# A delta net's projection fed without its norm factor, beta / |k|^2 moved into the decay's exponent, seven small transfers for fourteen

## The chip, the cores and the metric

One core of a Trainium2 chip runs the whole program. The metric is the time of one execution in device microseconds, as the median of three: 1213.83 before the change (1212.03 to 1216.12). The change touches the first 200 of these microseconds almost alone: the first layer, a gated delta net.

## The reference, cut to what matters

Two transformer blocks run one after the other over 256 tokens of 1024 features in fp32. Only the first layer of the first block matters here:

```
hn  = x * rsqrt(mean(x^2) + eps) * a_norm_w              # rmsnorm, one factor per token
q, k, v, z, b, a = split(hn @ a_w_in)                    # 1024, 1024, 2048, 2048, 16, 16 columns
q, k, v = silu(causal_conv4(q, k, v))                    # four taps along the tokens
q, k    = q / |q| * 128^-0.5, k / |k|                    # 8 heads, used by 16 value heads
beta, g = sigmoid(b), -exp(a_log) * softplus(a + dt_bias)
gc      = cumsum(g);  decay[c, s] = exp(gc[c] - gc[s])   # c >= s, inside a chunk of the tokens
m       = strict_lower(beta[c] * (k[c] . k[s]) * decay)
T       = inverse(1 + m)                                 # lower triangular
...                                                      # T and the products q.k, k.v make the outputs o
h       = x + (rmsnorm(o) * silu(z)) @ a_w_out
```

The factor of the norm is one number per token, so that (x * a_norm_w) @ W, times that number per token, is the projection too. In the same way |k|^-2 and beta are factors of m, and a positive factor of an exponential is a summand, its logarithm, in the exponent.

## The kernel before, in words

**Matmuls.** Features lie on the 128 partitions and tokens along the free axis, so the input is eight pieces of 128 features by 256 tokens. A product in fp32 is made of three matmuls in a faster format: each operand is split into a high half (a rounded copy) and a low half (what the rounding left), and high by high, low weight by high x and high weight by low x are summed in a PSUM bank (`mm3`, L247 to L251). All weights stream in as 362 chunks of 128 x 1024 (`wall[j]`), each of eight tiles of 128 x 128 in the order in which TensorE uses them. `_raw` issues a chunk's transfer on SyncE's queue, `_prep` makes the high half `wh` on ScalarE (L186) and the low half `wl` on VectorE (L187). There are four buffers of each kind, and `w` prepares two chunks ahead.

**Order.** The engines' orders are static. A scheduler makes them from the order in which the code issues the instructions and from priorities: the splits of the weights have a high one. `behind` adds an order between two instructions of an engine by hand. Work that isn't part of a weight loop runs in generators: `tick` (L200) advances each of them by one step for every four weight tiles that were used. A finished PSUM bank is evacuated by `evac`; while `ready` is false the evacuations wait in a queue, `evq`, and `flush` issues them.

**The start of the delta net (`gdn`, L547 to L574).** The input arrives in four transfers of two pieces (`h`), then the identity, chunk 0 and the table of small columns. ScalarE squares, VectorE sums, TensorE sums over the partitions (`colsum`, L361), VectorE takes the reciprocal root (`rstd`), TensorE spreads it over all partitions (`rows`). Then each piece is multiplied by a_norm and by the factor (L568), split into `xh` on ScalarE (L569) and `xl` on VectorE (L570), and the projection starts. Nine matmuls without use (`warm`) fill waits of TensorE.

**The projection.** First come two groups of k columns together, piece by piece (`ko=2` in `gemm`), then the 48 columns of b and a, the other two groups of k, and then by the table `ORDER` four groups of q, four blocks of z and eight groups of v. A group is a bank of two times 128 columns by 256 tokens. Its evacuation `conv` (L642 to L651) is one copy times the last tap's weight on ScalarE, three taps on VectorE for each half, each reading the bank, and a Silu on ScalarE. `evac_ba` (L605 to L628) makes beta and the running sums of g: Tanh, Exp and Ln on ScalarE and small operations on VectorE; its `later` turns them over into `bg`, with the tokens on the partitions.

**The decay.** `factors` makes 1/|k| and, in `negc`, -beta/|k|^2 (L685). `x_stage` (L692 to L720) then takes each of eight key heads: two matmuls make the products `kk` in three blocks of 128 columns (two in the first half of the tokens, one in the second), and for each of its two value heads two matmuls make the exponents in a bank `rp`, ScalarE takes three Exp with gc as the bias (L704 to L706), and VectorE multiplies `kk`, `negc` and the Exp in two instructions (L707, L708). Diagonal blocks go out to DRAM, come back in another shape, `inv_stage` inverts them in 31 steps on VectorE, and fourteen small transfers (L770, L773, all on SyncE) bring the results back. `levels` builds the whole inverse from them, and `chain` the outputs. `a_stage` (L732, L733) makes the products of q and k as `x_stage` does those of k.

Of the kernel before, what the change touches and what calls it, by code (L numbers as in the profile page):

```python
# [19 lines left out]
P = 128  # L20
# [92 lines left out]
WARM = (5, 1, 3)  # L113
# [19 lines left out]
PRE0 = 1  # L133
# [5 lines left out]
PINS = {1: 0, 3: 1}  # L139
# [3 lines left out]
class Builder:  # L143
# [113 lines left out]
    def gemm(self, name, x, K, ctiles, evac, ko=0):  # L257
# [170 lines left out]
    def split(self, hi, lo, src, scale=None, eng=None):  # L428

        nc = self.nc  # L430
        if scale is None:
            nc.scalar.activation(hi, src, AF.Copy)
            nc.vector.tensor_tensor(lo, src, hi.bitcast(F32), ALU.subtract)
# [71 lines left out]
    def run(self):  # L505
        nc, tc = self.nc, self.tc
        with ExitStack() as es:
# [9 lines left out]
            self.ident = self.cp.tile([P, P], F32, name="ident")  # L517
            for b in range(4):
# [4 lines left out]
            self.ones = self.cp.tile([P, P], F32, name="ones")  # L523
            nc.gpsimd.memset(self.ones, 1.0)
# [22 lines left out]
    def gdn(self):  # L547
# [3 lines left out]
        with tc.tile_pool(name="gp", bufs=1) as gp:  # L551

            wb = self.bank("warm")
            warm = lambda n, r: [nc.tensor.matmul(wb[:, 0 : r.shape[1]], self.ones, r, start=True, stop=True) for _ in range(n)]
            warm(WARM[0], self.ones)
            for b in range(4):
                self.add_sq(self.sqs, "sqa", b, lambda o: nc.scalar.activation(o, self.h[:, 2 * b : 2 * b + 2], AF.Square))
            nc.vector.tensor_tensor(self.sqs[0], self.sqs[0], self.sqs[1], ALU.add)
            cs = self.colsum(self.sqs[:1])
            if PRE0:  # L560
                self._prep(0)
            rc = self.rstd(cs, D)
            warm(WARM[1], self.sqs[0])
            rb = self.rows(rc, psum=True)
            warm(WARM[2], self.h[:, 0])
            for i in range(8):
                t = gp.tile([P, T], F32, tag="t2", bufs=8, name="xn")
                op = nc.vector.scalar_tensor_tensor(t, self.h[:, i], self.col("a_norm", i), rb, ALU.mult, ALU.mult)  # L568
# [7 lines left out]
    def gdn_body(self, gp, x):  # L576
# [28 lines left out]
        def evac_ba(g, b):  # L605
# [24 lines left out]
            def later():  # L630
                for _ in range(6):
                    yield
# [1324 lines left out]
```

## Time and profile before

| | us |
|---|---|
| median of three executions | 1213.83 (1212.03 to 1216.12) |
| the profiled execution, its own time | 1210.2 |
| its span | 1208.3 |
| TensorE busy | 1183.6 (98%) |
| VectorE busy | 895.0 (74%) |
| ScalarE busy | 687.2 (57%) |
| GpSimd busy | 20.4 (2%) |

The span is the time from the first instruction of the profiled execution to the last; its own time has what lies around the span as well. In the profile's rows TensorE is PE, its weight loads PEld, VectorE DVE, ScalarE ACT, GpSimd POOL and SyncE SP (its DMA queue SPq); L249 is line 249 of the kernel that the row belongs to. A row of a timeline gives the start, the length, the engine, the line, the operation, output <- inputs, and the shape; brackets at its end give the idle time of the engine just before and what ended it. Several instructions of a kind in a row stand in one row with x and their count. Matmuls are pipelined: the distance of two starts, and not the length, is what one costs.

### The profile page before, as it was taken

Reading aid. Unit: us, or ns where it says so; the run is one execution under the profiler, and the core shown is the slowest. Engines: PE = TensorE matmul, PEld = TensorE weight load, DVE = VectorE, ACT = ScalarE, POOL = GpSimd, SP = SyncE. Lnnn points to the kernel's source line nnn. Section 1 sums busy time; section 2 is a strip of 40 time slices with the busy share of each in tenths; the row PEclk is TensorE's granted clock in tenths of the full one; section 3 lists DMA queues with packets and bytes.
Section 4 is the critical chain, followed back from the end, with each engine's and each line's share of the span. In section 5 each row is a group of like instructions: output and inputs, shape, how many; then the busy total and the mean of one; then the engine's idle time right before and its main releaser. Section 6 shows DMA issues by size and latency. Waiting matters only on the chain.

```text
span 1208.3 us, 23419 instructions
## 1 busy us (share of the span) xinstructions
PE 1183.6 (98%) x9368; PEld 1120.2 (93%) x9368; DVE 895.0 (74%) x1680; ACT 687.2 (57%) x1170; POOL 20.4 (2%) x47
## 2 busy tenths in 40 slices
PE   7999999999999999989999999999999999999997
PEld 6989988999999999979999999889799999999996
DVE  6978977668877778879987878756656567655555
ACT  4785556546655556556655556754465545444443
POOL 1000000000000001000000000000000000000000
PEclk9999999999999999999999999999999999999999
DMA  6547365454655557434665565363255573555552
GB/s 223 180 131 218 120 202 179 143 166 156 208 189 178 189 177 246 133 106 150 203 190 181 190 190 161 114 200 123 88 174 175 177 239 124 176 187 182 189 181 81
DMA packets 68317, 206.01 MB, mean 170 GB/s; under 512 B 18197, under 2 KB 18341, under 8 KB 67952
## 3 DMA queue, kind: packets, MB, share of 16 engines
q1 hardware_dynamic: 65600, 194.77, 50.5%
q0 software_dynamic: 2608, 9.75, 2.3%
q8 instruction: 73, 1.20, 0.4%
q14 instruction: 36, 0.29, 0.1%
HBM read 199.75 MB, written 4.74 MB: 169 GB/s over the span
## 4 chain that ended last, share of the span: by engine, by line
PE 87%; DVE 7%; issue 3%; ACT 2%; DMA 1%; SPq 0%; POOL 0%; DVEq 0%; ACTq 0%; POOLq 0%
PE pb L249 20%; PE pb L250 19%; PE pb L251 19%; PE acc L249 7%; PE acc L250 7%; PE acc L251 7%; DVE wl L187 2%; DVE cy L650 1%; PE ssb L669 1%; DMA wzog<-wzd 0%; DMA ident<-cst 0%; ACT wh L186 0%; PE kv L1563 0%; PE csum L366 0%; PE pt L1159 0%
## 5 line engine op out<-in xcount | busy, mean ns | idle before, releaser
L187 DVE TENSOR_TENSOR wl<-wr,wh 128x1024 fp32r<-128x1024 f32 x362 | 442.0, 1224 | 198.2 <-ACT wh L186 196.8
L186 ACT ACTIVATE wh<-wr 128x1024 fp32r<-128x1024 f32 x362 | 381.8, 1057 | 337.0 <-issue 100.1
L249 PE MATMUL pb<-xh,wh 128*128 128x256 f32 x1224 | 347.8, 284 | 0.6 <-ACT xh L569 0.6
L251 PE MATMUL pb<-xh,wl 128*128 128x256 f32 x1224 | 345.7, 283 | 2.2 <-DVE wl L187 2.2
L250 PE MATMUL pb<-xl,wh 128*128 128x256 f32 x1224 | 345.3, 282 | 0.2 <-DVE xl L570 0.2
L249 PEld LDWEIGHTS pb<-xh,wh 128*128 128x128 f32 x1224 | 231.7, 189 | 2.8 <-issue 1.3
L251 PEld LDWEIGHTS pb<-xh,wl 128*128 128x128 f32 x1224 | 229.6, 188 | 2.6 <-DVE wl L187 2.6
L250 PEld LDWEIGHTS pb<-xl,wh 128*128 128x128 f32 x1224 | 230.2, 188 | 0.5 <-DVE xl L570 0.4
L249 PE MATMUL pb<-fh,wh 128*128 128x256 f32 x416 | 118.4, 285 | 0.0
L250 PE MATMUL pb<-fl,wh 128*128 128x256 f32 x416 | 117.4, 283 | 0.1
L251 PE MATMUL pb<-fh,wl 128*128 128x256 f32 x416 | 116.6, 281 | 0.0
L249 PE MATMUL acc<-ah,wh 128*128 128x256 f32 x352 | 98.7, 280 | 0.0
L251 PE MATMUL acc<-ah,wl 128*128 128x256 f32 x352 | 98.6, 280 | 0.0
L250 PE MATMUL acc<-al,wh 128*128 128x256 f32 x352 | 98.5, 280 | 0.0
L249 PEld LDWEIGHTS pb<-fh,wh 128*128 128x128 f32 x416 | 77.9, 188 | 1.4 <-issue 0.4
L250 PEld LDWEIGHTS pb<-fl,wh 128*128 128x128 f32 x416 | 78.2, 188 | 1.1 <-DVE fl L436 0.3
L251 PEld LDWEIGHTS pb<-fh,wl 128*128 128x128 f32 x416 | 78.8, 189 | 0.0
L998 DVE SCALAR_TENSOR_TENSOR fy<-fpad,cols,fy 128x256 f32<-128x256 f32 x176 | 73.6, 479 | 0.0
L249 PE MATMUL pb<-wh,xh 128*128 128x512 f32 (+1 forms) x176 | 70.5, 402 | 0.0
L250 PE MATMUL pb<-wl,xh 128*128 128x512 f32 (+1 forms) x176 | 68.1, 387 | 0.5 <-DVE wl L187 0.5
L251 PE MATMUL pb<-wh,xl 128*128 128x512 f32 (+1 forms) x176 | 68.0, 386 | 0.0
L249 PEld LDWEIGHTS acc<-ah,wh 128*128 128x128 f32 x352 | 66.8, 190 | 0.0
(437 smaller groups left out, 2089.2 us busy)
## 6 DMA issues: line engine op xcount, KB each, us to landing
wr<-wall SPq DMA_DIRECT2D x362, 512.0 KB, 3.6
wzd<-zt POOLq DMA_DIRECT2D x8, 256.0 KB, 3.0
wzog<-wzd POOLq DMA_DIRECT2D x4, 512.0 KB, 5.0
bias<-bd POOLq DMA_DIRECT2D x4, 512.0 KB, 7.1
h<-xT SPq DMA_DIRECT2D x4, 256.0 KB, 4.1
h<-xT POOLq DMA_DIRECT2D x1, 1024.0 KB, 8.0
wrow<-wrow POOLq DMA_DIRECT2D x1, 1024.0 KB, 10.2
out_dram<-mw SPq DMA_DIRECT2D x4, 256.0 KB, 2.0
```

The lines of the kernel that those rows point to most:

```text
L186: nc.scalar.activation(hi, r, AF.Copy)
L187: i = nc.vector.tensor_tensor(lo, r, hi.bitcast(F32), ALU.subtract)
L249: mm(out, ah, bh, start=start, stop=False, skip_group_check=skip)
L250: mm(out, ah, bl, start=False, stop=False, skip_group_check=skip)
L251: mm(out, al, bh, start=False, stop=stop, skip_group_check=skip)
L650: nc.vector.scalar_tensor_tensor(y[:, i, n:], u[:, : T - n], w(j), y[:, i, n:], ALU.mult, ALU.add)
L669: nc.tensor.matmul(ssb[:, c : c + 1], sq[:, i, tt * P : tt * P + P], self.ones[:, 0:1], start=True, stop=True)
L998: nc.vector.scalar_tensor_tensor(y[:, i], u[:, i, j : j + T], w(j), y[:, i], ALU.mult, ALU.add)
```

## The change

**The start.** The pieces of x are h times a_norm, without the factor; they are split right from `h`. The factor is made beside the projection by a generator, `norm`: nine ticks, the column sum and the reciprocal root into `rc`, four ticks, the row broadcast into `rb` (copied to SBUF), and only then are the evacuations let go. `conv` begins with one multiplication of the whole bank by `rb` into a tile `un` in SBUF, which the taps then read; `evac_ba` has one such multiplication too; `evac_z` scales its copy by `rc`. The first four chunks, the pieces of x and the squares have an order written by hand on ScalarE and VectorE, chunk 0 in two halves. The transfers on SyncE are now h0, chunk 0, h1, chunk 1, h2, chunk 2, h3, the columns; the identity is on GpSimd's queue and the norm's weights alone on ScalarE's. Thirteen warming matmuls replace nine. With `ko`, the four tiles of a piece are multiplied all high by high first, then all high weights by `xl`, then all low weights by `xh`, instead of tile by tile.

**The decay.** `lnc` is ln(max(beta, 1e-30) / |k|^2), added to gc in `bgc` and given to Exp as its bias. `kk` and the Exp lie in the same order of blocks, so that one instruction multiplies 384 columns, with -1 as the scalar. `bg` is made three ticks later.

**The transfers.** The kinds of blocks are the outer axis of `XA`, so the two halves of the tokens go in one transfer: seven for fourteen; and some copies of two halves in `levels` are one.

```diff
-WARM = (5, 1, 3)
+WARM = 13
+NA1, NA2 = 9, 4
...
             for k in range(K):
+                ts = []
                 for g in range(ko):
                     for i, c in enumerate(groups[g]):
-                        wh, wl = self.w(name, k * P, c * P)
-                        self.mm3(banks[g][:, i * T : i * T + T], wh, wl, xh[:, k], xl[:, k],
-                                 k == 0 and i == 0, k == K - 1, True)
+                        ts.append((banks[g][:, i * T : i * T + T], *self.w(name, k * P, c * P), k == 0 and i == 0))
+                mm = self.nc.tensor.matmul
+                for o, wh, wl, first in ts:
+                    mm(o, wh, xh[:, k], start=first, stop=False, skip_group_check=True)
+                for o, wh, wl, first in ts:
+                    mm(o, wh, xl[:, k], start=False, stop=False, skip_group_check=True)
+                for o, wh, wl, first in ts:
+                    mm(o, wl, xh[:, k], start=False, stop=k == K - 1, skip_group_check=True)
...
+            self.anw = self.cp.tile([P, KD], F32, name="anw")
+            nc.scalar.dma_start(self.anw, self.a["cols"][:, 0:KD])
             for b in range(4):
                 nc.sync.dma_start(self.h[:, 2 * b : 2 * b + 2], self.a["xT"][:, 2 * b : 2 * b + 2])
-            nc.sync.dma_start(self.ident, self.cst("ident"))
-            self._raw(0)
+                if b < 3:
+                    self._raw(b)
+            nc.gpsimd.dma_start(self.ident, self.cst("ident"))
...
-                op = nc.vector.scalar_tensor_tensor(t, self.h[:, i], self.col("a_norm", i), rb, ALU.mult, ALU.mult)
-                nc.scalar.activation(x[0][:, i], t, AF.Copy)
-                nc.vector.tensor_tensor(x[1][:, i], t, x[0][:, i].bitcast(F32), ALU.subtract)
...
+            def tile_(i):
+                act.append(nc.scalar.activation(x[0][:, i], self.h[:, i], AF.Copy, scale=self.anw[:, i : i + 1]))
+                dve.append(nc.vector.scalar_tensor_tensor(x[1][:, i], self.h[:, i], self.anw[:, i : i + 1], x[0][:, i].bitcast(F32), ALU.mult, ALU.subtract))
...
+            tile_(0)
+            part(0, lo)
+            tile_(1)
+            part(0, hi)
+            tile_(2)
+            tile_(3)
+            part(1, full)
+            s0 = square(0)
...
+            self.ready = False
+            def norm():
+                for _ in range(NA1):
+                    yield
+                self.rc = self.sp.tile([P, 2], F32, tag="rc", bufs=1, name="rc")
+                self.rstd(self.colsum([s0[:, 0]]), D, None, self.rc)
+                for _ in range(NA2):
+                    yield
+                self.rb = self.rows(self.rc)
+                self.ready = True
+                self.flush()
...
+            un = t2([P, 2, T], "un")
+            nc.vector.tensor_tensor(un, ev2(bank), self.bc2(self.rb), ALU.mult)
             y = t2([P, 2, T], "cy")
             for i in range(2):
-                u = bank[:, i * T : i * T + T]
+                u = un[:, i]
...
+                nc.scalar.activation(lnc, lnc, AF.Ln)
...
-                    nc.vector.scalar_tensor_tensor(XA[:, h, 0:2], ev2(kk[:, 0:T]), negc[:, h : h + 1], EA[:, h, 0:2], ALU.mult, ALU.mult)
-                    nc.vector.scalar_tensor_tensor(XA[:, h, 2], kk[:, T:384], negc[:, 16 + h : 17 + h], EA[:, h, 2], ALU.mult, ALU.mult)
+                    nc.vector.scalar_tensor_tensor(XA[:, h], ev3(kk), -1.0, EA[:, h], ALU.mult, ALU.mult)
...
-                for tt in range(2):
-                    Q[3].dma_start(XA[blk(b), :, 2 * tt, blk(b)], s3[b, tt].rearrange("h c i -> c h i"))
-                    if b < 3:
-                        c = (0, 32, 0)[b]
-                        Q[3].dma_start(T64[blk(b), tt, :, c : c + 32], s2[b, tt].rearrange("h i c -> i h c"))
+                Q[3].dma_start(XAb[blk(b), 0:2, :, blk(b)].rearrange("p k h c -> p (k h) c"), s3[b].rearrange("a h c i -> c (a h) i"))
+                if b < 3:
+                    c = (0, 32, 0)[b]
+                    Q[3].dma_start(T64[blk(b), :, :, c : c + 32].rearrange("p a h c -> p (a h) c"), s2[b].rearrange("a h i c -> i (a h) c"))
```

**The orders.** Three places show how the instructions now stand. Numbers behind names tell buffers apart; lines are those of either kernel.

ScalarE around the gates' Exp and Ln (`gr`) and the first Silu (`kT`), before:

```order
L186 ACTIVATE wh8_440<-wr8_347 128x1024
L647 ACTIVATE cy_334<-pb_212,cols_76 128x256
L613 ACTIVATE gcr_378<-gr_377 16x256
L615 ACTIVATE gr_377<-gr_377 48x256
L647 ACTIVATE cy_395<-pb_213,cols_76 128x256
L617 ACT_TABLE_LOAD
L617 ACTIVATE gr_377<-gr_377 48x256
L186 ACTIVATE wh9_483<-wr9_408 128x1024
L651 ACT_TABLE_LOAD
L651 ACTIVATE kT_204<-cy_334 128x512
```

ScalarE at the same place after the change (`un` is the bank times the factor):

```order
L185 ACTIVATE wh11_562<-wr11_485 128x1024
L722 ACT_TABLE_LOAD
L722 ACTIVATE kT_184<-cy_422 128x512
L682 ACTIVATE gcr_435<-gr_434 16x256
L732 ACTIVATE sqg_432<-kT_184 128x512
L684 ACT_TABLE_LOAD
L684 ACTIVATE gr_434<-gr_434 48x256
L718 ACTIVATE cy_455<-un_453,cols_76 128x256
L686 ACT_TABLE_LOAD
L686 ACTIVATE gr_434<-gr_434 48x256
```

The gates came ahead of the first Silu, in chunk 8's time; now they come behind it, in chunk 11's, and a Silu's table is loaded ahead of them.

VectorE from one chunk's low half to the next after the gates (`gch` is the gates' last result, `cy` a tap), before:

```order
L187 TENSOR_TENSOR wl9_484<-wr9_408,wh9_483 128x1024
L626 TENSOR_TENSOR gch_196<-gcr_378,gch_196 16x384
L650 SCALAR_TENSOR_TENSOR cy_395<-pb_213,cols_76,cy_395 128x255
L650 SCALAR_TENSOR_TENSOR cy_468<-pb_407,cols_76,cy_468 128x255
L650 SCALAR_TENSOR_TENSOR cy_395<-pb_213,cols_76,cy_395 128x254
L650 SCALAR_TENSOR_TENSOR cy_468<-pb_407,cols_76,cy_468 128x254
L650 SCALAR_TENSOR_TENSOR cy_395<-pb_213,cols_76,cy_395 128x253
L650 SCALAR_TENSOR_TENSOR cy_468<-pb_407,cols_76,cy_468 128x253
L187 TENSOR_TENSOR wl10_514<-wr10_438,wh10_513 128x1024
```

VectorE after the change, up to the low half of chunk 12:

```order
L721 SCALAR_TENSOR_TENSOR cy_455<-un_453,cols_76,cy_455 128x255
L695 TENSOR_TENSOR gch_175<-gcr_435,gch_175 16x384
L721 SCALAR_TENSOR_TENSOR cy_455<-un_453,cols_76,cy_455 128x254
L721 SCALAR_TENSOR_TENSOR cy_472<-un_470,cols_76,cy_472 128x255
L721 SCALAR_TENSOR_TENSOR cy_455<-un_453,cols_76,cy_455 128x253
L721 SCALAR_TENSOR_TENSOR cy_472<-un_470,cols_76,cy_472 128x254
L721 SCALAR_TENSOR_TENSOR cy_472<-un_470,cols_76,cy_472 128x255
L721 SCALAR_TENSOR_TENSOR cy_472<-un_470,cols_76,cy_472 128x253
L721 SCALAR_TENSOR_TENSOR cy_472<-un_470,cols_76,cy_472 128x254
L713 TENSOR_TENSOR un_545<-pb_484,rowb_418 128x512
L721 SCALAR_TENSOR_TENSOR cy_472<-un_470,cols_76,cy_472 128x253
L186 TENSOR_TENSOR wl12_593<-wr12_515,wh12_592 128x1024
```

Six taps and the gates' last operation stood between the low halves of chunks 9 and 10; now nine taps, a multiplication by the factor and the same operation of the gates stand right ahead of the low half of chunk 12.

TensorE where the decay begins (`ssb` is a sum of squares of k, `kk` the products, `rp` the exponents, `pb` the projection), before:

```order
L669 MATMUL ssb_206<-ones_86,sqg_559 128x1 x4
L698 MATMUL kk_751<-kT_204 128x256
L699 MATMUL kk_751<-kT_204 128x128
L702 MATMUL rp_754<-gch_196,identr_190 128x384
L703 LDWEIGHTS identb_189
L703 MATMUL rp_754<-mask3b_188,identb_189 128x384
L702 MATMUL rp_762<-gch_196,identr_190 128x384
L703 LDWEIGHTS identb_189
L703 MATMUL rp_762<-mask3b_188,identb_189 128x384
L249 MATMUL pb_715<-wh13_641,xh_88 128x512
```

TensorE after the change:

```order
L740 MATMUL ssb_186<-ones_78,sqg_723 128x1 x4
L778 MATMUL rp_797<-gch_175,identr_169 128x384
L779 LDWEIGHTS identb_168
L779 MATMUL rp_797<-mask3b_167,identb_168 128x384
L774 MATMUL kk_816<-kT_184 128x2x128
L775 MATMUL kk_816<-kT_184 128x128
L778 MATMUL rp_819<-gch_175,identr_169 128x384
L779 LDWEIGHTS identb_168
L779 MATMUL rp_819<-mask3b_167,identb_168 128x384
L778 MATMUL rp_826<-gch_175,identr_169 128x384
L779 LDWEIGHTS identb_168
L779 MATMUL rp_826<-mask3b_167,identb_168 128x384
```

Before, two exponents follow the first products and z's matmuls go on behind them, with chunk 13; now the decay begins behind z's block with chunk 16, the first exponents stand ahead of the products, and the second head's products follow in the same place.

## Rows read from the trace of the kernel before

**Rows 1.** The page: busy time, share of the span and instructions of each engine.

```profile
PE 1183.6 (98%) x9368; PEld 1120.2 (93%) x9368; DVE 895.0 (74%) x1680; ACT 687.2 (57%) x1170; POOL 20.4 (2%) x47
```

**Rows 2.** Stages: stretch, length, then PE, PEld, DVE, ACT, POOL busy us, clock, DMA share, GB/s.

```profile
30.00:60.00 30.00, 30.00 (x247) 29.55 (x245) 28.56 (x59) 22.38 (x35) 0.00 (x0) 1.00 0.57 183
...
112.00:160.00 48.00, 45.35 (x323) 41.85 (x321) 47.65 (x119) 26.42 (x43) 0.00 (x0) 1.00 0.51 153
```

**Rows 3.** Timeline of TensorE: start, length, engine, line, operation, tiles, shape, [idle before, releaser].

```profile
9.18 1.01 PE L366 MATMUL csum<-ones,sqa 128*128 128x1 f32 x4 [5.68 <-DVE sqa L558]
...
14.88 0.50 PE L249 MATMUL pb<-xh,wh 128*128 128x256 f32 x2 [0.59 <-ACT xh L569]
...
15.89 0.28 PE L249 MATMUL pb<-xh,wh 128*128 128x256 f32 x1
16.01 0.28 PE L250 MATMUL pb<-xl,wh 128*128 128x256 f32 x1
...
22.75 0.38 PE L251 MATMUL pb<-xh,wl 128*128 128x256 f32 x1 [0.69 <-DVE wl L187]
...
75.08 0.28 PE L249 MATMUL pb<-xh,wh 128*128 128x256 f32 x1
```

**Rows 4.** Timeline of ScalarE: where it waits for arrivals, and three pieces of x.

```profile
4.00 0.63 ACT L557 ACTIVATE sqa<-h 128x512 f32<-128x512 f32 x1 [1.99 <-DMA h<-xT]
...
8.54 1.06 ACT L186 ACTIVATE wh<-wr 128x1024 fp32r<-128x1024 f32 x1 [1.08 <-DMA wr<-wall]
...
11.85 1.06 ACT L186 ACTIVATE wh<-wr 128x1024 fp32r<-128x1024 f32 x1 [0.22 <-DMA wr<-wall]
...
16.08 1.01 ACT L569 ACTIVATE xh<-xn 128x256 fp32r<-128x256 f32 x3
```

**Rows 5.** Timeline of VectorE: first evacuation, gates, last product of the decay, inversion.

```profile
29.14 1.23 DVE L187 TENSOR_TENSOR wl<-wr,wh 128x1024 fp32r<-128x1024 f32 x1 [3.04 <-ACT wh L186]
30.28 0.99 DVE L650 SCALAR_TENSOR_TENSOR cy<-pb,cols,cy 128x255 f32<-128x255 f32 x2
...
32.72 0.53 DVE L611 TENSOR_SCALAR gr<-pb,cols 48x256 f32<-48x256 f32 x1
...
41.29 0.55 DVE L626 TENSOR_TENSOR gch<-gcr,gch 16x384 fp32r<-16x384 f32 x1
...
88.67 0.34 DVE L708 SCALAR_TENSOR_TENSOR XA<-kk,fac,EA 128x128 f32<-128x128 f32 x1
...
101.74 0.19 DVE L757 TENSOR_TENSOR fst<-NT,TI 128x31 f32<-128x31 f32 x1
```

**Rows 6.** Groups by line and shape, first 245 us: instructions, busy us, mean ns, idle before.

```profile
L650 DVE SCALAR_TENSOR_TENSOR cy<-pb,cols,cy 128x255 f32<-128x255 f32 x32 | 15.1, 477 | 3.5 <-ACT cy L647 3.2
...
L707 DVE SCALAR_TENSOR_TENSOR XA<-kk,fac,EA 128x256 f32<-128x256 f32 x16 | 7.7, 480 | 3.6 <-ACT EA L705 3.4
...
L708 DVE SCALAR_TENSOR_TENSOR XA<-kk,fac,EA 128x128 f32<-128x128 f32 x16 | 5.5, 343 | 2.0 <-ACT EA L706 2.0
```

**Rows 7.** VectorE in the feed-forward stage: the factor's multiplication, and a group of taps.

```profile
304.62 0.69 DVE L991 TENSOR_TENSOR fpad<-pb,rowb 128x512 f32<-128x512 f32 x1
...
L998 DVE SCALAR_TENSOR_TENSOR fy<-fpad,cols,fy 128x256 f32<-128x256 f32 x60 | 25.3, 480 | 0.0
```

**Rows 8.** Timeline of ScalarE: a table load between Exp and Ln; three Exp of a head.

```profile
34.53 1.28 ACT L617 ACT_TABLE_LOAD   x1
35.82 0.42 ACT L617 ACTIVATE gr<-gr 48x256 f32<-48x256 f32 x1
...
69.72 0.38 ACT L704 ACTIVATE EA<-rp,bg 128x128 f32<-128x128 f32 x1
69.97 0.39 ACT L705 ACTIVATE EA<-rp,bg 128x128 f32<-128x128 f32 x1
```

**Rows 9.** Timeline of SyncE: first and last of the small transfers behind the inversion.

```profile
154.32 0.38 SPq L773 DMA_DIRECT2D h<-s  x1
...
161.26 1.09 SPq L770 DMA_DIRECT2D XA<-s  x2
```

More of the change, by code (lines that the diff above doesn't have):

```diff
@@ L432, in split @@
             nc.scalar.activation(hi, src, AF.Copy)
[L433 removed]
+            self.last = nc.vector.tensor_tensor(lo, src, hi.bitcast(F32), ALU.subtract)
         else:
@@ L553, in gdn @@
             wb = self.bank("warm")
[L554 to L567, printed above, removed]
-                op = nc.vector.scalar_tensor_tensor(t, self.h[:, i], self.col("a_norm", i), rb, ALU.mult, ALU.mult)
-                nc.scalar.activation(x[0][:, i], t, AF.Copy)
-                nc.vector.tensor_tensor(x[1][:, i], t, x[0][:, i].bitcast(F32), ALU.subtract)
-                if i in PINS:
-                    self.pins[PINS[i]] = op
-                    self._prep(PINS[i])
+            for _ in range(WARM):
+                nc.tensor.matmul(wb[:, 0:P], self.ones, self.ones, start=True, stop=True)
@@ new lines, in square, with add, chunk @@
+            def square(b):
+                t = gp.tile([P, 2, T], F32, tag="t2", bufs=8, name="sq")
+                act.append(nc.scalar.activation(t, self.h[:, 2 * b : 2 * b + 2], AF.Square))
+                return t
+            def add(o, a_, b_):
+                dve.append(nc.vector.tensor_tensor(o, a_, b_, ALU.add))
+            raws = {}
+            def chunk(j):
+                self._raw(j)
+                raws[j] = self.raws.pop(j)
+                self.raws[j] = None
+                self.halves[j] = (self.wtile(j, F32R, "wh"), self.wtile(j, F32R, "wl"))
@@ new lines, in gdn @@
+            for j in range(3):
+                chunk(j)
+            lo, hi, full = slice(0, 512), slice(512, 1024), slice(0, 1024)
+            tile_(0)
[6 more added lines that the diff above has]
+            s0 = square(0)
+            tile_(4)
+            tile_(5)
+            s1_ = square(1)
+            chunk(3)
+            add(s0, s0, s1_)
+            part(2, full)
+            s2_ = square(2)
@@ new lines, in gdn @@
+            tile_(6)
+            tile_(7)
+            s3_ = square(3)
+            self._raw(4)
+            add(s0, s0, s2_)
+            part(3, full)
+            add(s0, s0, s3_)
+            add(s0[:, 0], s0[:, 0], s0[:, 1])
+            for l in (act, dve):
+                for p, n in zip(l, l[1:]):
+                    self.behind(n, p)
+            self.dvl = dve[-1]
+            self.ready = False
[9 more added lines that the diff above has]
+                self.flush()
@@ L574, in gdn @@
+            self.side(norm())
             self.gdn_body(gp, x)
@@ L630, in later @@
             def later():
-                for _ in range(6):
+                for _ in range(9):
                     yield
@@ L856, in yz2 @@
             if qz is not None:
-                for tt in range(2):
-                    nc.vector.tensor_copy(XA[lo, h4(qz), 2 * tt, hi], vz[lo, tt])
+                nc.vector.tensor_copy(XAb[lo, 0:2, h4(qz), hi], vz[lo])
                 st["lev"] += 1
```

81 lines of the change are left out of this document (45 added, 36 removed).

## The prediction

> **What bounds the kernel now.** I read the page's busy shares first: TensorE is busy 98% of the span and VectorE 74% [rows 1], so only a stretch where TensorE waits can give time back, and a saving elsewhere counts only if TensorE waits for it. Then the table of stages: in the delta net VectorE is busy 28.56 of 30 us from 30 to 60 and 47.65 of 48 from 112 to 160, and TensorE loses 2.65 us in the second [rows 2]. So there are two stretches in which VectorE has nothing to spare, with a looser one between. Last, TensorE's own timeline: it waits 5.68 us for the sum of squares, starts the projection at 14.88, and waits 0.69 us more at 22.75 [rows 3]. The start is the prize: some 14 us in which little is multiplied.
>
> All times below are span times of the one profiled execution (span 1208.3, its own time 1210.2, 1.9 us around the span). That execution is 3.6 us under the median of the three runs, 1213.83, so I add the difference that I find to the median.
>
> **The start: 9.2 us gained.** The norm leaves the path; the first matmul needs one piece of the input and half a weight chunk. Arrivals come from bytes and landings: 0.25 MB had landed at 4.00, 1.6 MB at 8.54, 2.9 MB at 11.85 [rows 4]. In the new order the weight chunks stand at 0.75, 1.5, 2.25 and 3.3 MB, so by interpolation they land at about 5.9, 8.3, 10.2 and 13. ScalarE spends 1.06 on a chunk, 0.34 on a piece of x (three in 1.01) and 0.63 on a square [rows 4]; half a chunk is 0.6, so the first matmul comes at 6.5. Matmuls of 256 columns start 0.12 apart [rows 3], so eight of the stream's tiles (one chunk, 24 matmuls) take 2.88. ScalarE has chunk 1 split by 9.4, chunk 2 by 12.3 and chunk 3 by 15.2 (it does pieces and squares between), VectorE follows 1.14 behind each [rows 5], and with the new grouping (four high, four low-x, four low-w) TensorE waits little: chunks 0 to 3 end at 18.4. Before they end at 14.88 + 0.6 for the first pieces + 96 x 0.12 + 0.7 waited = 27.6. Bounds: 7 (the small transfer of the norm's weights lands late, which no row shows) to 10.
>
> **The first full stretch: 9.6 us of it given back.** The factor must still be made: column sum and row broadcast now stand in TensorE's stream, the broadcast after chunk 6, hence at 18.4 + 3 x 2.88 = 27, and the first evacuation starts at 27.9. Before it began at 30.28 on VectorE [rows 5]. So all evacuations keep their old clock time while TensorE is 9.2 us further on, and VectorE has more to do. From 27.9 to the low half of chunk 12 the new order puts 18 taps (0.42 each: 477 ns, less what neighbours overlap), 3 low halves (1.14: 29.14 to 30.28, 0.09 under their length), 4 new multiplications by the factor (0.60: the same operation in the feed-forward stage is 0.69 long) and the gates' twelve small operations, which took 4.4 together, the first at 32.72 and the last at 41.29, and gain one of about 0.45 [rows 5 to 7]. That is 7.6 + 3.4 + 2.4 + 4.9 = 18.3. Two table loads are new on ScalarE, because the first Silu is now ahead of Tanh and Exp: each took 1.28 [rows 8], and VectorE's next gate operations stand behind Exp and Ln: 2.7 us. Chunk 12 is ready at 27.9 + 18.3 + 2.7 = 48.9. TensorE reaches it at 18.4 + 8 x 2.88 + 1.8 (sums, broadcast, transposes) = 43.2, has 2.4 us of later work that was drawn forward, and waits 3.2. Chunk 13 comes 11 taps, one multiplication and one low half later, at 55.3: 1.7 more. The next wait is for the decay. The z block ends at about 67.8 (matmuls of 512 columns: 0.24, twice the pitch of 256). Behind it ScalarE evacuates z (1.1), splits a chunk (1.0), loads a table, takes Ln, loads a table, and has three Exp done at 73.7 (0.25 apart [rows 8]). TensorE has only two banks left, to 69.5, and then waits for these Exp: 4.2 and 0.8. So chunk 17 starts at 76.3. Before it starts right behind the z block, at 75.08 [rows 3], plus 0.8 for one sum that by then only the changed kernel has done: 75.9. The four waits are 9.9 and the two moved jobs 0.75, some 1 us more than the positions allow; I take the positions: net so far **+0.4**, nothing left of the gain. Bounds: -4 (if ScalarE and VectorE reach each step 4 us sooner) to +4.
>
> [...] A table load in the trace takes 1.28 and the next activation starts 0.01 after it [rows 8]. [...] The taps read a bank before and SBUF after; rows: 477 ns from the bank, 480 from SBUF for one element more [rows 6, 7], so I give the copy no gain. [...]
>
> **The looser stretch: 0.** The decay's products are one instruction for 384 columns in place of 480 + 343 ns [rows 6]; by the slope between the two sizes it costs 0.53 against 0.66 overlapped, 16 times: 2.1 us of VectorE. They wait for ScalarE's Exp, 16 heads x 0.75 from 73 and two chunks between: the last product comes at about 88, before at 88.67 [rows 5]. So the inversion of 31 steps, behind the transfers, starts as before near 101.7 or 0.5 sooner.
>
> **The second full stretch: +2.0.** Eight evacuations of v add 8 x 0.60 = 4.8 to VectorE, the merged query products take off 6 x 0.13 = 0.8: 4.0 more in a stretch with 0.35 us idle [rows 2]. So between +4.0 (nothing covers it, and TensorE's 2.65 us of waits grow by all of it) and 0 (all deferred past 160, where nothing waits); I take the middle, 2.0.
>
> **The rest: 0.** Seven transfers fewer: the 14 issues stand 0.53 us apart on SyncE from 154.32 to 161.26 [rows 9], so the queue is free 3.7 us sooner; the levels that read them begin later than these landings and TensorE loses little there. Bounds -1 to 0. The feed-forward stages also get the new grouping for their first banks; no wait in them is long enough to matter: -0.3 to +0.3.
>
> **Sum.** -9.2 + 9.6 + 2.0 = +2.4: span 1210.7, its own time 1212.6, and on the median **1216.2**.
>
> **The rivals.**
> - *The start is kept in part (25%).* VectorE and ScalarE get through the first full stretch 5 us sooner than I walk it, and the second one's 2.0 is covered. For it: VectorE is idle 4 us before 27.9, and my walk puts every dependency of a queue in series. Against it: 28.56 of 30 us busy. Cap: the inversion starts only behind the transfers of the products, so no more than 3 to 5 us stay at the levels. Time: 1213.8 - 9.2 + 4.6 + 0 = 1209.2, under 1210.2.
> - *The multiplications by the factor are paid in both full stretches (19%), slower.* Place: the low halves, queued behind evacuations on VectorE. Price: 14 of the 16 multiplications fall there (4 k, 2 q, 8 v), 14 x 0.60 = 8.4 us; it decides where no idle time covers them: 4.0 instead of 2.0 in the second stretch and 4 instead of 0.4 in the first. Time: 1213.8 + 2.4 + 2.0 + 3.6 = 1222.
> - *A switch of tables costs twice its row (3%)*: four on the path x 1.28 more [rows 8]: 1221.3. No row of before shows such a gap.
> [...]
>
> The forecast itself has 50%, with its own range 1212 to 1220.
>
> **How the numbers follow.** A change under 0.3% (3.6 us) can't be told from none: 1210.2 to 1217.5. Faster: the first rival, and a little of the forecast's lower tail, 0.25. Slower: the second and the third, 0.22, and about a quarter of the forecast's range, 0.11: 0.33. Same: 0.42. The range reaches past the first rival and to the second: 1207 to 1222.
>
> **What would show it.** First projection matmul near 6.5; chunks 0 to 3 done near 18; the first multiplication by the factor near 28; TensorE waiting for a low half near 45 to 49 and 53 to 55, and for Exp near 70 to 74; last product of the decay near 88; VectorE full from 112 to 160 with TensorE losing more than 2.65 there. I am wrong if TensorE has no wait over 2 us between 20 and 76 (then the start is kept), or if the first matmul comes after 9.

## The result, and the profile after

The changed kernel takes 1222.23 us (median of 6, 1221.48 to 1224.71) against 1213.2 (6 runs) of the kernel before: a ratio of 1.0079, 95% interval 1.0067 to 1.0091. It is 9.0 us slower where 2.4 were forecast, and 0.2 us over the forecast's range. The profiled execution has a span of 1220.5, 12.2 over that of before.

The page first (busy time, share of the span, instructions), and from its second part the granted clock of TensorE in 40 slices, in tenths of full speed (a 9 is 90% or more), last the same row of the kernel before:

```profile
PE 1195.1 (98%) x9376; PEld 1131.2 (93%) x9376; DVE 895.9 (73%) x1652; ACT 690.7 (57%) x1171; POOL 20.8 (2%) x48
...
PEclk9889999999999999989999999999999999999999
...
PEclk9999999999999999999999999999999999999999
```

TensorE is busy as large a share as before [rows 1], but for 11.5 us more. The clock's row points at the reason: two of the first four slices have an 8, and one near the middle; in the kernel before all 40 digits are 9, and in steps of 1 us its clock is at 1.00 from the start to 1204, behind TensorE's last matmul. The stages, in the columns of [rows 2]:

```profile
30.00:60.00 30.00, 25.54 (x172) 24.23 (x170) 26.06 (x54) 20.89 (x32) 0.00 (x0) 0.83 0.30 93
112.00:160.00 48.00, 45.55 (x349) 43.19 (x348) 47.18 (x121) 25.59 (x40) 1.08 (x2) 1.00 0.44 143
```

From 30 to 60 us TensorE is busy 25.54 of 30 and its mean clock is 0.83; in [rows 2] both were full. VectorE, 28.56 us busy there before, now has 26.06: it isn't fuller, it waits too. The second stretch, from 112 to 160, looks as it was: 47.18 against 47.65 for VectorE, and TensorE loses 2.45 us where it lost 2.65. But the work in it comes some 9.6 us later now (below); from 121.6 to 169.6, which has about the same work, VectorE is busy all 48.00 us and TensorE loses 2.87. TensorE alone in steps of 2 us (busy time, clock, DMA share, GB/s) shows where the clock fell:

```profile
44.00:46.00 2.00, 1.46 (x9) 1.00 0.00 0
46.00:48.00 2.00, 0.00 (x0) 0.90 0.00 0
48.00:50.00 2.00, 1.73 (x6) 0.50 0.00 0
...
54.00:56.00 2.00, 2.00 (x10) 0.50 0.00 0
...
80.00:82.00 2.00, 1.34 (x4) 0.50 0.46 184
```

The clock is at 1.00, falls near 47.6, within the wait that ends at 48.27, and stays at 0.50 for some 10 us. All stretches of half clock in the delta net together (47 to 58, 61 to 65, 78 to 86) are 20 us long. TensorE's timeline around them, as in [rows 3]:

```profile
6.76 0.74 PE L270 MATMUL pb<-xh,wh 128*128 128x256 f32 x4
...
45.08 0.38 PE L775 MATMUL kk<-kT 128*128 128x128 f32 x2
48.27 0.66 PE L778 MATMUL rp<-gch,identr 128*128 128x384 f32 x1 [2.81 <-DVE un L713]
...
51.54 0.41 PE L249 MATMUL pb<-xl,wh 128*128 128x256 f32 x1
51.76 0.41 PE L250 MATMUL pb<-xh,wl 128*128 128x256 f32 x1
...
59.83 1.05 PE L740 MATMUL ssb<-ones,sqg 128*128 128x1 f32 x8 [1.65 <-ACT sqg L732]
...
76.71 0.38 PE L775 MATMUL kk<-kT 128*128 128x128 f32 x2
80.66 0.69 PE L778 MATMUL rp<-gch,identr 128*128 128x384 f32 x1 [3.56 <-ACT EA L782]
...
84.62 0.66 PE L248 MATMUL pb<-xh,wh 128*128 128x256 f32 x1
```

The first matmul comes at 6.76; three waits follow: 2.81 us before the first exponents, 1.65 before a sum of squares and 3.56 before the fifth exponents. After the first of them two matmuls of 256 columns start 0.22 us apart, where 0.12 is their distance in [rows 3]. The last row is chunk 17's first matmul. VectorE, as in [rows 5]:

```profile
28.78 0.69 DVE L713 TENSOR_TENSOR un<-pb,rowb 128x512 f32<-128x512 f32 x1 [0.99 <-ACT rowb L428]
...
44.67 2.85 DVE L721 SCALAR_TENSOR_TENSOR cy<-un,cols,cy 128x254 f32<-128x254 f32 x7
47.44 0.68 DVE L713 TENSOR_TENSOR un<-pb,rowb 128x512 f32<-128x512 f32 x1
...
48.43 1.22 DVE L186 TENSOR_TENSOR wl<-wr,wh 128x1024 fp32r<-128x1024 f32 x1
...
96.95 1.01 DVE L783 SCALAR_TENSOR_TENSOR XA<-kk,EA 128x384 f32<-128x384 f32 x2
...
111.36 0.19 DVE L831 TENSOR_TENSOR fst<-NT,TI 128x31 f32<-128x31 f32 x1 [0.86 <-DMA NT<-s]
```

Seven taps and the multiplication `un` stand in front of what TensorE waits for at 48.27 (`un` frees a bank). The last product of the decay starts after 96.95, before at 88.67, and the inversion at 111.36, before at 101.74: 9.6 us late. From there on both kernels take about the same time; the first matmul of the levels, before and after:

```profile
163.82 0.24 PE L826 MATMUL y1p<-h,XA 32*32 32x32 f32 x2
...
173.51 0.24 PE L899 MATMUL y1p<-h,XA 32*32 32x32 f32 x2
```

The first multiplication by the factor in the feed-forward stage comes at 289.33 and 299.46. So nearly all that the change costs is lost before the inversion starts; some 2 us of the span's difference come behind a wait of the attention stage (below, e10). Groups by line and shape, as in [rows 6]:

```profile
L721 DVE SCALAR_TENSOR_TENSOR cy<-un,cols,cy 128x255 f32<-128x255 f32 x32 | 14.8, 479 | 3.7 <-ACT cy L718 3.5
...
L713 DVE TENSOR_TENSOR un<-pb,rowb 128x512 f32<-128x512 f32 x16 | 11.0, 685 | 2.6 <-PE pb L250 1.5 <-ACT rowb L428 1.0
L783 DVE SCALAR_TENSOR_TENSOR XA<-kk,EA 128x384 f32<-128x384 f32 x16 | 8.8, 556 | 7.0 <-ACT EA L782 6.9
```

A tap from SBUF takes 479 ns, from the bank 477; the multiplication 685; a product of 384 columns 556. The forecast's 0.53 was for the distance of two such products: the two at 96.95 take 1.01 together. The transfers behind the inversion, first and last, as in [rows 9]:

```profile
165.25 0.32 SPq L846 DMA_DIRECT2D h<-s  x1
...
172.78 0.83 SPq L843 DMA_DIRECT2D XA<-s  x1
```

The seven hold the queue for 8.4 us, from 165.25 to 173.61; the fourteen before held it for 8.0, from 154.32 to 162.35. The queue is not free sooner, as the forecast had it: the seven take up to 1.3 us each to issue, where 0.49 was usual.

### The profile page after: what moved, and what is told of

The parts are those of the page before. It is cut to its first block, busy times and chain, and to the rows that moved or that the text cites. A ratio compares the mean times of both kernels' runs of the same rounds, so it can differ in the third digit from the quotient of the medians.

```text
span 1220.5 us, 23397 instructions
## 1 busy us (share of the span) xinstructions
PE 1195.1 (98%) x9376; PEld 1131.2 (93%) x9376; DVE 895.9 (73%) x1652; ACT 690.7 (57%) x1171; POOL 20.8 (2%) x48
## 4 chain that ended last, share of the span: by engine, by line
PE 83%; DVE 8%; ACT 4%; issue 3%; DMA 1%; POOL 0%; DVEq 0%; SPq 0%; ACTq 0%; POOLq 0%
PE pb L248 18%; PE pb L249 17%; PE pb L250 17%; PE acc L248 7%; PE acc L249 7%; PE acc L250 7%; DVE wl L186 2%; DVE cy L721 1%; DMA wr<-wall 1%; PE pb L274 1%; PE pb L270 1%; PE pb L272 1%; ACT wh L185 1%; PE ssb L740 1%; PE pt L1230 1%
## 5 line engine op out<-in xcount | busy, mean ns | idle before, releaser
L186 DVE TENSOR_TENSOR wl<-wr,wh 128x1024 fp32r<-128x1024 f32 x358 | 437.1, 1223 | 202.6 <-ACT wh L185 201.2
L185 ACT ACTIVATE wh<-wr 128x1024 fp32r<-128x1024 f32 x358 | 377.2, 1056 | 340.7 <-issue 103.5
L248 PE MATMUL pb<-xh,wh 128*128 128x256 f32 x1112 | 317.5, 286 | 0.0
L250 PE MATMUL pb<-xh,wl 128*128 128x256 f32 x1112 | 315.6, 284 | 0.7 <-DVE wl L186 0.7
L249 PE MATMUL pb<-xl,wh 128*128 128x256 f32 x1112 | 314.7, 283 | 0.0
L248 PEld LDWEIGHTS pb<-xh,wh 128*128 128x128 f32 x1112 | 211.7, 190 | 1.8 <-issue 1.3
L250 PEld LDWEIGHTS pb<-xh,wl 128*128 128x128 f32 x1112 | 209.9, 189 | 0.9 <-DVE wl L186 0.9
L249 PEld LDWEIGHTS pb<-xl,wh 128*128 128x128 f32 x1112 | 210.3, 189 | 0.1
```

Source lines behind the costliest of these rows:

```text
L185: nc.scalar.activation(hi, r, AF.Copy)
L186: i = nc.vector.tensor_tensor(lo, r, hi.bitcast(F32), ALU.subtract)
L248: mm(out, ah, bh, start=start, stop=False, skip_group_check=skip)
L249: mm(out, ah, bl, start=False, stop=False, skip_group_check=skip)
L250: mm(out, al, bh, start=False, stop=stop, skip_group_check=skip)
```

## The experiments

Three theories were set against each other. C: the waits are much as forecast, but behind each of them TensorE runs at half clock (granted 0.50). V: VectorE's queue with the new multiplications sets the pace, and the clock only fills time that is lost anyway. T: the loads of tables and the logarithm on ScalarE hold the decay back. Each kernel ran beside the kernel before on the same chip; ratios are to that.

One caution for the stages below: the kernel of e10 has the instructions of the kernel before up to the attention stage, and yet its profile has the start of the inversion at 102.68, the first matmul of the levels at 165.68 and the feed-forward stage's first multiplication at 292.18, where the profile of before has 101.74, 163.82 and 289.33. So two profiles of the same work lie 1 to 3 us apart, and a smaller difference between single profiles shows nothing.

**e1: fill the waits.**

```diff
+                    for _ in range({("kss", 3): 3}.get((key, g), 0)):
+                        nc.tensor.matmul(ssb[:, 384:512], self.ones, self.ones, start=True, stop=True)
...
+                for _ in range({0: 6, 2: 7}.get(j, 0)):
+                    nc.tensor.matmul(kk[:, 384:512], self.ones, self.ones, start=True, stop=True)
```

The first loop stands ahead of a sum of squares, the second behind the products `kk`.

> The changed kernel with 16 matmuls without use added where TensorE waited in its profile: 6 in front of the first exponents (it waited 2.81 us at 45.4), 3 in front of the fourth sum of squares (1.65 at 57.9) and 7 in front of the fifth exponents (3.56 at 76.9). They write columns of a bank that nobody reads; the other instructions keep their order. Theory C (the forecast's waits are right, but behind each of them TensorE runs at half clock, granted 0.50 from 48 to 56, 62 to 64 and 80 to 84): no stretch of half clock behind the filled waits, 4 to 7 us sooner than the changed kernel, 1215 to 1218, 1.002 to 1.004 of the kernel before. Theory V (VectorE's queue with the new multiplications sets the pace, and the clock only fills waits that are there anyway): within 1.5 us of the changed kernel, 1221 to 1224, with the waits longer by what the clock gave back. Theory T (the table loads and the logarithm on ScalarE): no change either.

1218.6 us, 1.0045 (1.003 to 1.0061): some 4 us back, with 16 matmuls more and the same work; just over C's 1215 to 1218 and well under V's 1221 to 1224. Waits of 1.47, 1.19 and 2.00 us were left, since a filling matmul took no more than 0.24 us. The clock held behind the first wait (the sum of squares behind it starts at 55.83, in the changed kernel at 59.83) and fell behind the others (58 to 62 and 78 to 82):

```profile
58.00:62.00 4.00, 4.00 (x13) 0.57 0.80 236
78.00:82.00 4.00, 4.00 (x18) 0.59 0.00 1
```

**e5: fill them whole.** 11 behind the first `kk`, 14 behind the third, 7 behind the second exponents.

> As e1_fill, with enough matmuls to cover the whole waits: a filling matmul took some 0.22 us at full clock, so 11 ahead of the first exponents, 7 behind the second exponents and 14 ahead of the fifth. Theory C: no half clock at all in the delta net (10 us of it were left to e1_fill there, about 7 without the attention stage), so 2 to 3.5 us sooner than e1_fill: 1215 to 1217, 1.001 to 1.003 of the kernel before, the forecast's +2.4. Theory V (the waits alone cost it): as e1_fill, 1218 to 1219.

1216.29 us, 1.0028 (1.0018 to 1.0038), as C said. Filling matmuls and chunk 17 in TensorE's timeline, then its clock from 40 to 90, then the last product of the decay and the start of the inversion on VectorE:

```profile
45.27 2.62 PE L777 MATMUL kk<-ones 128*128 128x128 f32 x22
48.24 0.41 PE L780 MATMUL rp<-gch,identr 128*128 128x384 f32 x1 [0.35 <-DVE un L713]
...
78.38 0.38 PE L248 MATMUL pb<-xh,wh 128*128 128x256 f32 x1
```

```profile
40.00:60.00 20.00, 18.79 (x143) 1.00 0.23 68
60.00:90.00 30.00, 29.41 (x187) 1.00 0.51 155
```

```profile
90.44 1.01 DVE L787 SCALAR_TENSOR_TENSOR XA<-kk,EA 128x384 f32<-128x384 f32 x2
...
104.00 0.19 DVE L835 TENSOR_TENSOR fst<-NT,TI 128x31 f32<-128x31 f32 x1
```

In the first wait TensorE does 2.62 us of nothing useful and waits 0.35, and it goes on at 48.24, where it did at 48.27; nothing else is changed, and the inversion starts 7.4 us sooner (104.00 against 111.36). No half clock is left in the delta net. That is the test on which C rests: with the clock up, the same waits cost about what the forecast's sum said (its terms are looked at below).

**e2: the factor sooner, by ticks.** `NA1, NA2 = 6, 2` for `9, 4`.

> The changed kernel with the factor made sooner: 6 and 2 ticks in place of 9 and 4, so that the first multiplication by the factor comes some 6 us sooner, near 22 instead of 28.8. Theory C: the low halves are done sooner, the wait near 45 falls under 1 us and the clock stays up there: 1214 to 1217; the wait for the exponents near 77 may stay. Theory V: the whole 6 us of VectorE in the first full stretch come back and none in the second: 1216 to 1218. Theory T: the exponents come as late as before, 1220 to 1222.

1218.61 us, 1.0034 (1.0018 to 1.0051): in none of the three ranges, and what happened isn't what any of them said. TensorE's two matmuls of the factor:

```profile
19.15 0.61 PE L372 MATMUL csum<-ones,sq 128*128 128x1 f32 x4
...
26.19 1.22 PE L424 MATMUL rowp<-dg,ones 128*128 128x128 f32 x4 [3.46 <-DVE dg L422]
```

The sum is 2.4 us sooner than at 21.51, yet the broadcast waits 3.46 for VectorE, where low halves stand between the small operations: the first multiplication came at 27.87 instead of 28.78. The wait moved ahead, and the fall of the clock with it: behind it, from 27.43 to 31.48, matmuls of 256 columns start 0.21 apart, ahead of it 0.12. No wait over 1 us was left near 45, and that near 77 stayed. So e2 says nothing on a factor that is sooner.

**e6: the factor sooner, by order.** Ticks 6 and 3; the low halves of chunks 6 and 7 are put behind the factor's last operations.

```diff
+                self.pins[6] = self.rcl
...
+                self.pins[7] = self.dgl
```

`rcl` is the last operation of the reciprocal root, `dgl` the one that makes the broadcast's operand.

> The changed kernel with the factor truly sooner (in e2_early its small operations stood behind low halves, and it came at 27.5): 6 and 3 ticks, and the low half of chunk 6 behind the last small operation of the factor by hand. The factor then is at all partitions near 24.5 in place of 28.7. Theory V (what the first full stretch costs is the late start of VectorE): 4 us of the wait for it come back, the wait near 45 to 48 under 1 us, 1214.5 to 1216.5, if the clock stays up as well. Theory T (the chain of tables and logarithm before the first Exp): the wait near 77 stays with its half clock, 1217 to 1219 as e2_early.

1217.53 us, 1.0035 (1.0022 to 1.0047): the first multiplication at 24.53, 4.2 us sooner, and yet a wait for a low half and half clock behind it (0.50 from 44 to 50):

```profile
44.10 0.58 PE L250 MATMUL pb<-xh,wl 128*128 128x256 f32 x1 [2.04 <-DVE wl L186]
```

The wait for the exponents stayed at 3.56, with half clock behind it (the exponents' first matmul 0.69 long, 0.42 ahead of the wait). V's 1214.5 to 1216.5 was missed, but so was its condition, a wait under 1 us near 45; T's number came.

**e4: the decay as before.** `negc` for `lnc`, two products for each head, Exp with gc alone as its bias.

> The changed kernel with the decay as before: -beta/|k|^2 as a scalar on VectorE in two products for each head, no logarithm and one table load less ahead of the first Exp. Theory T: the wait near 77 falls from 3.6 to about 1 us, and with it the half clock behind it: 1216 to 1219. Theory V: 16 x 0.13 + 16 x 0.13 us more on VectorE, the second in its second full stretch: 1222 to 1225. Theory C: the first fall of the clock stays, the second one goes: 1217 to 1221.

1218.52 us, 1.0036 (1.0023 to 1.0048), within T's range and C's and under V's. The wait near 77 and the half clock behind it are gone; one of 1.93 us ends at 141.87, with a fall of the clock behind it (a matmul of 256 columns is 0.42 long at 142.97, 0.28 at 142.68), where the kernel before has one of 1.46 and no fall. ScalarE's first Exp:

```profile
60.38 0.37 ACT L775 ACTIVATE EA<-rp,bg 128x128 f32<-128x128 f32 x1
```

It comes at 60.38; in the changed kernel at 79.72. The kernel before has it at 61.09:

```profile
61.09 0.37 ACT L704 ACTIVATE EA<-rp,bg 128x128 f32<-128x128 f32 x1
```

The changed kernel's rows show why:

```profile
76.89 1.28 ACT L761 ACT_TABLE_LOAD   x1
78.18 0.23 ACT L761 ACTIVATE fac<-fac 128x32 f32<-128x32 f32 x1
78.43 1.28 ACT L780 ACT_TABLE_LOAD   x1
79.72 0.37 ACT L780 ACTIVATE EA<-rp,bgc 128x128 f32<-128x128 f32 x1
```

Exp now needs the logarithm, the logarithm needs 1/|k|, and so no exponent can be taken before all four groups of k have their sums; before, only the products waited for 1/|k|. In these rows a switch of tables takes no more than its load: Ln starts 0.01 after a load of 1.28, as the activation in [rows 8] does, and the next load 0.02 after Ln's end.

**e8: the decay's part alone, in the kernel before.**

> The kernel before with the decay's part alone: beta/|k|^2 by a logarithm in the exponent, one product of 384 columns for each head, the start and the transfers as before. Theory T: the two table loads and the logarithm stand ahead of the first Exp: 2.8 us of wait and half clock behind it, 3 to 5 us slower: 1217 to 1219. Theory V: 16 x 0.13 us less for VectorE in the second full stretch: 0 to 2 us faster, 1212 to 1214.

1212.66 us, 0.9995 (0.9985 to 1.0005): no change, against T's 3 to 5 us, and within V's 1212 to 1214. Its first Exp:

```profile
73.33 0.37 ACT L710 ACTIVATE EA<-rp,bgc 128x128 f32<-128x128 f32 x1
```

Here too the first Exp comes 12 us later, and the inversion at 105.86 (4.1 late), but the levels come at 164.87, no later than in e10's profile. TensorE waited only 1.0 us, at 74, and the clock held (1.00 up to 200). So the later exponents cost little by themselves; with the new start they end a wait of 3.56 us with half clock behind it.

**e7: e6 and e4 together.**

> e6_soon with the decay of the kernel before (e4_nodecay's part). If the three losses are apart (late factor, chain of the logarithm, half clock behind each), both gains add: 3.5 to 5 us for the decay as in e4_nodecay and 3 to 6 for the factor: 1210 to 1214, 0.997 to 1.000 of the kernel before. If VectorE's work alone sets the pace (theory V), no better than e6_soon.

1213.62 us, 1.0000 (0.999 to 1.0011). The two gains add, but for some 1 us, and V, by which it should have been no better than e6, missed. First multiplication by the factor and start of the inversion:

```profile
24.43 0.69 DVE L717 TENSOR_TENSOR un<-pb,rowb 128x512 f32<-128x512 f32 x1 [0.27 <-ACT rowb L428]
...
100.88 0.19 DVE L832 TENSOR_TENSOR fst<-NT,TI 128x31 f32<-128x31 f32 x1 [0.85 <-DMA NT<-s]
```

TensorE is some 8 us ahead at the start; the inversion is only 0.9 sooner than before, less than two profiles differ.

**e3: without the factor's multiplications.** The taps read the bank, so q, k and v lack the factor.

> The changed kernel without the 16 multiplications of a bank by the norm's factor: the taps read the bank as in the kernel before, so q, k and v lack the factor. Theory V: 14 x 0.60 = 8.4 us less on VectorE in the two full stretches, 1213 to 1215. Theory C: the wait near 45 gets shorter by the 4 multiplications ahead of it (2.4 us), the clock stays up there, and the second full stretch gets 4.8 us back on VectorE: 1212 to 1216, with granted clock 1.00 from 40 to 60. Theory T: 1218 to 1222, since the loads of tables stay.

1212.83 us, 0.9987 (0.9977 to 0.9998), 9 us or more under the changed kernel. The time fits C's 1212 to 1216 and all but fits V's 1213 to 1215, so it doesn't part the two. C's full clock from 40 to 60 was missed: in its profile there is still half clock from 45 to 49 and 72 to 80 (0.68 from 44 to 48, 0.50 from 73 to 79). So the multiplications cost time that the clock alone doesn't account for. From the inversion to the levels it took 59.4 us, the changed kernel 62.15 and the kernel before 62.08.

**e12: without the factor and with the old decay.** Of the change the start and the transfers are left.

> The changed kernel with the decay of before and without the 16 multiplications by the factor (q, k and v lack it): of the whole change the new start and the seven transfers are left. If the start's 8 to 9 us are lost to the factor's multiplications and the chain of the logarithm, they are to be seen here: inversion near 93 to 95, 1205 to 1208. If VectorE's and ScalarE's order in the first full stretch holds the decay back whatever TensorE does: inversion near 99 to 101, 1210 to 1213.

1209.91 us, 0.9984 (0.997 to 0.9998), between the two ranges of the expectation and close to the second. TensorE's clock behind its waits at 42 to 45, and the inversion:

```profile
43.00:53.00 10.00, 8.81 (x40) 0.53 0.44 128
```

```profile
103.85 0.18 DVE L826 TENSOR_TENSOR fst<-NT,TI 128x31 f32<-128x31 f32 x1
```

Not 93 to 95: without any multiplication by the factor the inversion comes no sooner than before, in a profile with half clock from 43 to 53. That profile is of one of its slowest runs (1214.77); where the inversion starts in a fast one isn't shown. The 11 runs of this one program also show what goes with the clock: three with a mean granted clock of 0.997 took 1208.6 to 1208.8, two with 0.989 took 1214.8 and 1215.0. That is 6.2 us between runs of the same instructions; what else differed between them no run shows.

**e9: fourteen transfers.**

> The changed kernel with fourteen small transfers behind the inversion instead of seven. The forecast gave the seven no gain (0, bounds 0 to 1 us): as the changed kernel, 1221 to 1223. Rival: the queue that is free sooner is worth up to 3.7 us: 1224 to 1226.

1223.8 us, 1.0086 (1.0072 to 1.01) against 1.0079 (1.0067 to 1.0091): no difference that can be told, in four runs whose median lies between the two ranges. The rival had no chance to show: the seven transfers didn't free the queue sooner.

**e10: the attention stage, in the kernel before.**

```diff
             pv()
+            for _ in range(9 if g == 2 else 0):
+                nc.tensor.matmul(pt[:, 384:512], self.ones, self.ones, start=True, stop=True)
```

> The kernel before with 9 matmuls without use in the attention stage, in the 1.95 us for which TensorE waits at 531.2 for the split of the third group's output; nothing else is changed. In five of the profiles so far half clock follows this wait for 3.4 us or more, in that of the kernel before it doesn't. If half clock behind such a wait has its price in the kernel before too: no half clock there, 1 to 2.5 us faster, 1210.5 to 1212, and less spread among its runs. If the clock there costs nothing: 1212.5 to 1214.

1211.75 us, 0.9991 (0.9981 to 1.0001): within the 1210.5 to 1212 expected, but the interval includes no change at all. In the changed kernel the wait and the clock behind it are

```profile
543.32 0.58 PE L248 MATMUL acc<-oh,wh 128*128 128x256 f32 x1 [1.97 <-ACT oh L438]
```

```profile
543.00:549.00 6.00, 5.68 (x26) 0.50 0.26 91
```

With the filling matmuls the wait is gone and the clock stays at 1.00. The profile of the kernel before has the same wait, 1.95 us, and full clock behind it.

**e11: e7 with 9 filling matmuls at either place.**

> e7_soon_nodecay with 9 filling matmuls in its wait near 42 and 9 in the attention stage's wait (as e10_b_attn). Theory C: no half clock at all; 1.7 us for the first (3.4 us at half clock) and 1 to 2 for the second: 1209.5 to 1211.5, 0.997 to 0.998 of the kernel before, faster than both. If the inversion alone sets the end of the delta net (it began at 100.9 there, 101.7 in the kernel before), only the second counts: 1211 to 1213.

1211.72 us, 0.9987 (0.9978 to 0.9996): faster than both kernels, and than the one before by only some 1.6 us. That is just over C's 1209.5 to 1211.5 and within the other branch, 1211 to 1213. TensorE's busy time and clock in the attention stage (528 to 540):

```profile
528.00:540.00 12.00, 10.92 (x89) 1.00 0.42 133
```

No half clock is left before TensorE's last matmul. The inversion starts at 99.52, 2.2 sooner than before, and the levels at 163.92, no sooner: the second branch, by which the delta net's end doesn't follow TensorE, fits better.

## Why the prediction was wrong

**What held.** First matmul 6.76 (6.5 forecast); the first four chunks done near 19 (18.4); the first multiplication at 28.78 (27.9); chunk 12's low half done at 49.65 (48.9); a wait for Exp of 3.56 us (4.2, and 0.8 that didn't come); each table load its row (1.28); taps from SBUF no quicker (479 ns, from the bank 477). Near 45 the forecast's sign came, a wait for VectorE's queue of 2.81 us (3.2), but it was for the bank that `un` frees and not for the low half behind it. One wait agrees by luck: the forecast had 1.7 us for chunk 13's low half near 53 to 55, and there was none there; the 1.65 at 59.83 is for a square on ScalarE.

**The step that failed** is in the first full stretch: "The four waits are 9.9 ... net so far +0.4". Each wait was priced at its own length, and the matmuls between the waits at 0.12, the distance in [rows 3], and for 512 columns at twice that, 0.24 (0.23 in the trace of before). All these rows come from a profile in which the clock never falls while TensorE works; the forecast didn't say that its distances hang on that. Behind the waits they were 0.22 and 0.43 apart, for 20 us. So chunk 17 came at 84.62 instead of 76.3; in e5, with the clock up, at 78.38. The same step fails once more in the looser stretch: "the last product comes at about 88" became 96.95, in e5 90.44, and the inversion, "as before near 101.7", 111.36 and 104.00. Of the 9.6 us there 7.4 are thus the clock's, shown by e5; the 2.3 left are what the waits and all else before the inversion cost, which the forecast had at 0.4 for chunk 17 and at nothing for the inversion.

The medians say the same. e5 is 1.0028 of the kernel before, 2.2 to 4.6 us; the forecast's sum without the clock was +2.4. The sums agree, the terms don't: +0.4 and +2.0 were forecast ahead of the inversion and behind it, and in e5's profile the inversion is 2.3 late. The two spans are 7.8 apart (1220.5 and 1212.7). An estimate from the distances above: at half clock 0.10 of every 0.22 us is lost, so the 20 us of half clock in the changed kernel's delta net, where e5 has none, would cost some 9 us. In some 3 of the 20 TensorE stood still; without them it is some 8, against the 7.4 between the two starts of the inversion.

**Three errors with little weight.** [Rows 8] show an Exp at 69.72, but the first one before was at 61.09, and the forecast didn't ask where it stood. The time of the later exponents was about right with the clock up (the first three done at 73.7 in the forecast, at 75.42 in e5), but that they are later than before was not seen: e4 and e8 show that this part of the change, harmless alone, makes the longest wait together with the new start. Then the second full stretch was given +2.0 us; from the inversion to the levels both kernels take the same (62.08 and 62.15, and e10's profile 63.0). By e3 the multiplications cost 2.7 there; e8, with the merged products and no multiplication, took 59.0, 3.1 less than before. The single parts don't add up so simply in e4 (62.3) and e12 (62.6), so this is no more than two differences that agree. And the transfers gained nothing, as forecast, but not for the reason given: the queue that was to be free 3.7 us sooner wasn't.

**The rivals.** The second rival's time, 1222, was met, but by its mechanism only in part: 14 multiplications on VectorE, with 4.0 us lost in the first stretch and 4.0 in the second. From the inversion to the levels nothing was lost, and e5 took 6 us off with all of them in place. Yet the multiplications aren't free: one stands in the queue that TensorE waits for at 48.27, and e3 without them is 9 us or more quicker, beyond e5's 6, though 10 us of half clock are left in its delta net. They help to make the waits, and the clock makes the waits dear; the runs don't split this further. None of the rivals named the clock.

**Where the start's gain went.** TensorE has done the first four chunks at 19.00, before at 27.9. This lead of some 9 us is still there when it comes to the wait that ends at 48.27, and then turns into waits, since nothing of what it waits for starts sooner: the factor, the gates and the exponents follow VectorE and ScalarE. e7 and e11 recover the loss, not the gain: their inversion starts 0.9 and 2.2 us sooner than before, hardly more than two profiles differ. In e12, without the multiplications, some 4 us of the start at most reach the end (its runs at 0.997 against 1212.5, the median of 38 runs of the kernel before at 0.997 and 0.998).

**What stays open** is why the clock falls behind one wait and not behind another like it: in the kernel before 1.46 us without a fall (ended at 139.35), in e1 1.19 with one, and the attention stage's two waits, 0.91 and 1.97 us in the changed kernel and 0.93 and 1.95 in the kernel before, with 0.50 behind them in the profiles of the changed kernel, e7, e8, e9 and e12 and 1.00 in that of the kernel before.

## What to carry to other kernels

Where a change lets TensorE run ahead, ask what it will wait for, and price such a wait at its length plus what the matmuls behind it lose at half clock (here, of 256 columns, 0.22 us apart for 0.12, for 4 to 10 us); a trace of before without a fall of the clock has no row for that. If a wait can't be avoided, matmuls without use in it are worth trying: in e5 they gave back 6 us, and the work behind them began no later. And a factor moved into an exponent makes the exponential wait for all that the factor needs.

## What the runs showed of the hardware

The same program has runs that differ by 6 us with the mean granted clock of the run: 1208.6 at 0.997 and 1215.0 at 0.989 (e12). In 78 timed runs of the kernel before, the 18 with a mean of 0.998 have a median of 1212.5, the 5 with 0.994 one of 1217.2. So the granted clock goes with part of the scatter of a kernel's times; that single falls behind waits make it is likely, not shown. The profile of before (1210.2, no fall) was quicker than each of the 78 (1210.8 or more). Filling matmuls of 128 columns in fp32 took 0.24 us each (22 records in 2.62 us).
